# Retention layer: operands of the first two chunk steps made during the last block products, normalisation ahead of the state copy where heads change, and one residual load moved

## The chip, the cores and the metric

The program runs on one core of a Trainium2 chip. The metric is the device time of one execution in microseconds (us); lower is better. TensorE is written PE in the profile, its weight loads PEld, VectorE DVE, ScalarE ACT, GpSimd POOL; SyncE is SP, and it only issues transfers here. Each of these runs its own instructions in the order in which they stand in its queue, and an instruction that has to wait holds everything behind it on that engine. ACT issues a few transfers as well.

## The reference, cut to what matters

Two layers on a prompt of 1024 tokens and on 8 single decode tokens: a retention layer, then sliding-window attention. The change lies in the retention layer of the prompt, with 4 heads, keys of 256, values of 512 and chunks of 128 tokens (8 chunks a head):

```python
def step(S, inp):
    qc, kc, vc = inp
    inner = jnp.einsum('bthd,bshd->bhts', qc, kc) * dmask[None]
    o = jnp.einsum('bhts,bshe->bthe', inner, vc) \
        + jnp.einsum('bthd,bhde->bthe', qc, S) * cross_decay[None, :, :, None]
    S_new = S * chunk_decay[None, :, None, None] \
        + jnp.einsum('bshd,bshe->bhde', kc * k_decay[None, :, :, None], vc)
    return S_new, o
...
o = rmsnorm(o, g_out.reshape(RET_HEADS, RET_DV)).reshape(B, L, RET_V)
o = o * jax.nn.silu(gate)
return x + o @ w_out, S.astype(S0.dtype)
```

S starts at zero, so the first chunk of a head needs no product with the state.

## The kernel before, in words

All large products are in a split form: a float32 operand is a rounded part "h" and a remainder "l", and a product is three matmuls (h by h, h by l, l by h). Three stages follow one another.

**Block products (the input projection).** The projection to q, k, v and gate is made in a seven-product block scheme (`SEQ7`, L308). A list of slots gives PE's order: a slot is 12 matmuls of one block product (L330 to L332). `later(n, fn)` hangs work on slot n. The other engines evict each product (`evac`, L354 to L371), apply silu to the gate (L374), and SP spills q/k, v and gate to scratch in DRAM (`qks`, `vsc`, `gsc`; L387 is the spill of the gate). The last gate set passes through tiles named `raw`. Ten slots ahead of the end `b_first` (L750) issues the loads of q, v and gate of steps 0 and 1, of q of step 2, and of the masks.

**Chunk steps.** `steps` (L729) lists 32 steps: heads 0 and 1 in turn over their 8 chunks (steps 0 to 15), then heads 2 and 3. Steps 0, 1, 16 and 17 are first chunks (9 matmuls), the others have 15. The loop at L1052 writes, in round i: `b_qk(i+1)` (scores L859 and transposed keys L100 into a PSUM tile `tr`), `b_mm(i)` (state products L918 to L920 into `S`, output products L922 to L931 into `po`), the loads of q(i+3) and v(i+2), then `others(i)`, `b_tr(i-1)` (four transposes of the normalised output `on`, also into `tr`), and the load of gate(i+2). There are two `tr` tiles, used in turn.

`others(i)` (L1032) is the order of ACT, DVE and POOL: for step i-1 the state copies `b_Sh` (ACT, L938) and `b_Sl` (DVE, L950), then the norm `b_sq` (ACT, L957), `b_ts` (DVE, L961), `b_pw` (POOL, L115) and `b_on` (DVE, L969); for step i+1 the conversions `b_sT` (DVE), `b_vh` (ACT, L891), `b_kh` (ACT, L866), `b_kl` (DVE, L871), `b_sh` (ACT), `b_vl` (POOL, L896), `b_sl` (POOL); for step i-2 the gating `b_og` and the split `b_oh`/`b_ol`. After a head's last chunk `b_Sh` writes the final state to a tile `sf` (L942), which ACT sends to the output (L943).

Ahead of the loop SP issues `gbl(0)` and `gbl(1)`, the norm's gain rows of heads 0 and 1 (`gbh`, L996), and a mask `M23` (L1051). ACT issues `gbl(2)` and `gbl(3)` in rounds 16 and 17. The two `gbh` tiles and other tiles of this stage take memory in which the spilled `raw` tiles lay.

The last rounds also make the first output tile (128 features by 512 tokens) from its own weight rows (`b_w`, `b_wc`, `b_wmm`): 48 matmuls, L1024 to L1026, into a PSUM tile `S`.

**Output projection.** After `se.close()` (L1080) only PE's order is the written one; a scheduler places the instructions of SP, ACT, DVE and POOL. `wslot` (L1107) loads weights in pieces of 512 KB into two raw buffers `wr` (L1114), casts each on DVE to `wh` (L1121) and subtracts on POOL to `wl` (L1122). `ro_part` runs the matmuls L1179 to L1181 (12 for each piece in the first tiles). `ro_finish` (L1185) loads a tile of the residual x (`xr`, L1191), adds it to the product by transposing it into the same PSUM tile (L100), and writes x1 out. At the start stand `ro_ahead(2)` (the first four pieces) and `ro_finish(0, 0)`, which finishes the tile that the chunk stage made, and then the tile (1, 0).

Of the kernel before, what the change touches and what calls it, by code (L numbers as in the profile page):

```python
# [18 lines left out]
H = 4  # L19
# [51 lines left out]
def _trunk(ctx, tc, nc, a):  # L71
# [677 lines left out]

    def b_first():  # L750
# [98 lines left out]
    maskT = [M01[:, 0:128], M01[:, 128:256], M23[:, 0:128], M23[:, 128:256]]  # L849
    kdec = M01[:, 256:288].rearrange("p (h c) -> p h c", h=H)  # L850
    epsg = M01[:, 288:292]


    def b_qk(h, c):
        d = heads[h]
        qk = d["l", c][0]
        pt = d["pt", c] = trp.tile([128, 512], F32, name="tr")
        for f in range(2):
            mm(pt[:, :128], qk[:, 2 + f, :], qk[:, f, :], start=(f == 0), stop=(f == 1))  # L859
        for f in range(2):  # L860
            tr(pt[:, 128 + f * 128:256 + f * 128], qk[:, 2 + f, :], ident)

    def b_kh(h, c):
        d = heads[h]
        d["kh", c] = rp.tile([128, DK], F32R, name="kh", bufs=2)
        act(d["kh", c], d["pt", c][:, 128:384], AF.Copy, scale=kdec[:, h, c:c + 1])  # L866

    def b_kl(h, c):
        d = heads[h]
        d["kl", c] = rp.tile([128, DK], F32R, name="kl", bufs=2)  # L870
        dve.scalar_tensor_tensor(d["kl", c], d["pt", c][:, 128:384], kdec[:, h, c:c + 1], d["kh", c].bitcast(F32), MUL, SUB)  # L871

    def b_sT(h, c):
        d = heads[h]
        d["sT", c] = rp.tile([128, 128], F32, name="sT", bufs=2)
        dve.tensor_tensor(d["sT", c], d["pt", c][:, :128], maskT[h], MUL)

    def b_sh(h, c):
        d = heads[h]
        d["sh", c] = rp.tile([128, 128], F32R, name="sTh", bufs=2)  # L880
        act(d["sh", c], d["sT", c], AF.Copy)

    def b_sl(h, c):
        d = heads[h]
        d["sl", c] = rp.tile([128, 128], F32R, name="sTl", bufs=2)
        pool.tensor_tensor(d["sl", c], d["sT", c], d["sh", c].bitcast(F32), SUB)

    def b_vh(h, c):
        d = heads[h]
        d["vh", c] = rp.tile([128, DV], F32R, name="vh", bufs=2)  # L890
        act(d["vh", c], d["l", c][1], AF.Copy)  # L891

    def b_vl(h, c):
        d = heads[h]
        d["vl", c] = rp.tile([128, DV], F32R, name="vl", bufs=2)
        pool.tensor_tensor(d["vl", c], d["l", c][1], d["vh", c].bitcast(F32), SUB)  # L896

    def b_qh(h, c):
        d = heads[h]
        if c > 0:  # L900
            d["qh", c] = rp.tile([128, 2, 128], F32R, name="qh", bufs=2)
            dve.tensor_copy(d["qh", c], d["l", c][0][:, 0:2, :])

    def b_ql(h, c):
        d = heads[h]
        if c > 0:
            d["ql", c] = rp.tile([128, 2, 128], F32R, name="ql", bufs=2)
            pool.tensor_tensor(d["ql", c], d["l", c][0][:, 0:2, :], d["qh", c].bitcast(F32), SUB)
# [106 lines left out]

    def b_wmm(i):
# [11 lines left out]
    def at_step(fn, i):  # L1028
        if 0 <= i < len(steps):
            fn(*steps[i])  # L1030
# [21 lines left out]
    for i in range(-1, NS + 2):  # L1052
# [8 lines left out]
        if i in (NS - 2, NS - 1):  # L1061
            b_w(i - NS + 4)
# [872 lines left out]
```

## Time and profile before

| | |
|---|---|
| median of 3 runs | 1350.39 us (1350.27 to 1351.85) |
| the profiled execution | 1350.44 us, span 1348.6 us |
| mean granted TensorE clock | 0.995 |
| PE busy | 1308.8 us (97%) |
| PEld busy | 1222.4 us (91%) |
| POOL, DVE, ACT busy | 707.4, 701.1, 633.6 us |
| chunk stage and first output tile | from 542.8 to 703.6 us |

Positions are us from the start of the span. A timeline row gives start, duration, engine, line, operation, tile written and tiles read; a bracket at its end gives the engine's idle time ahead of it and what the profile takes for the releaser. A row with "SPq" or "ACTq" is the issue of a transfer, not the transfer. In a windows row each engine has its busy time and the number of its instructions; "PEclk" is the granted share of TensorE's clock, "DMA" the mean busy share of the 16 DMA engines.

### The profile page before, as it was taken

How to read it: one execution, taken by the hardware profiler on the slowest of the kernel's cores; microseconds unless marked ns; L12 is line 12 of the kernel's file. 1: busy time of each engine (PE TensorE's matmuls, PEld its weight loads, DVE VectorE, ACT ScalarE, POOL GpSimd, SP SyncE). 2: the span in 40 equal slices, each digit the busy share in tenths (PEclk: the TensorE clock that was granted, in tenths of full speed). 3: DMA queues.
4: the chain of work that ended last, by engine and by line, in shares of the span. 5: the costliest groups of instructions: out<-in, count | busy, mean ns of one | idle time of the engine just before them, and what ended most of it. 6: DMA issues, size and time to landing. Idle time of an engine off the chain costs nothing.

```text
span 1348.6 us, 25951 instructions
## 1 busy us (share of the span) xinstructions
PE 1308.8 (97%) x9661; PEld 1222.4 (91%) x9661; DVE 701.1 (52%) x1365; ACT 633.6 (47%) x1565; POOL 707.4 (52%) x825
## 2 busy tenths in 40 slices
PE   6999999999999999899999999998999999999998
PEld 6999999999999999787877899997889999998998
DVE  6943655656566553676752113335456555669321
ACT  5532444544455553677751112235465656656321
POOL 6653534435435543698977545454375666555000
PEclk9999999999999999999999999999999999999999
DMA  6314777587676753556556434442121111113532
GB/s 221 103 55 140 218 222 225 161 242 233 187 237 187 233 177 107 169 171 212 182 160 196 153 121 136 143 119 72 38 62 44 48 46 46 34 34 107 159 86 80
DMA packets 194771, 187.68 MB, mean 139 GB/s; under 512 B 12645, under 2 KB 174493, under 8 KB 194629
## 3 DMA queue, kind: packets, MB, share of 16 engines
q1 hardware_dynamic: 156576, 147.29, 35.9%
q10 hardware_dynamic: 38068, 38.73, 9.1%
q8 instruction: 76, 1.25, 0.4%
q14 instruction: 51, 0.41, 0.1%
HBM read 129.61 MB, written 57.41 MB: 139 GB/s over the span
## 4 chain that ended last, share of the span: by engine, by line
PE 85%; DVE 5%; POOL 4%; issue 3%; DMA 2%; ACT 1%; ACTq 0%; SPq 0%; POOLq 0%; DVEq 0%
PE b L330 7%; PE b L332 7%; PE b L331 7%; PE pj L1132 7%; PE pj L1134 6%; PE pj L1133 6%; PE b L323 4%; PE b L324 4%; PE b L325 4%; PE tr L100 4%; PE pj L1181 4%; PE pj L1179 4%; PE pj L1180 4%; PE o L1600 2%; POOL wl L1122 1%
## 5 line engine op out<-in xcount | busy, mean ns | idle before, releaser
L330 PE MATMUL b<-xh,woh 128*128 128x258 f32 x784 | 223.3, 285 | 0.0
L332 PE MATMUL b<-xh,wol 128*128 128x258 f32 x784 | 221.6, 283 | 0.0
L331 PE MATMUL b<-xl,woh 128*128 128x258 f32 x784 | 221.2, 282 | 0.0
L1132 PE MATMUL pj<-A_hi,wh 128*128 128x384 f32 (+1 forms) x512 | 178.7, 349 | 0.0
L1134 PE MATMUL pj<-A_hi,wl 128*128 128x384 f32 (+1 forms) x512 | 165.2, 323 | 0.0
L1133 PE MATMUL pj<-A_lo,wh 128*128 128x384 f32 (+1 forms) x512 | 165.1, 323 | 0.0
L330 PEld LDWEIGHTS b<-xh,woh 128*128 128x128 f32 x784 | 148.0, 189 | 4.1 <-issue 2.5
L331 PEld LDWEIGHTS b<-xl,woh 128*128 128x128 f32 x784 | 148.8, 190 | 0.0
L332 PEld LDWEIGHTS b<-xh,wol 128*128 128x128 f32 x784 | 148.1, 189 | 0.0
L221 POOL TENSOR_TENSOR wol<-raw,woh 128x512 fp32r<-128x512 f32 x52 | 68.5, 1325 | 139.7 <-ACT woh L216 139.0
L1122 POOL TENSOR_TENSOR wl<-wr,wh 128x1024 fp32r<-128x1024 f32 (+1 forms) x60 | 114.2, 1913 | 40.2 <-DVE wh L1121 19.5
L324 PE MATMUL b<-wol,xh 128*128 128x256 f32 x448 | 126.1, 281 | 0.3 <-DVE wol L221 0.3
L323 PE MATMUL b<-woh,xh 128*128 128x256 f32 x448 | 126.3, 282 | 0.0
L325 PE MATMUL b<-woh,xl 128*128 128x256 f32 x448 | 125.7, 281 | 0.0
L1132 PEld LDWEIGHTS pj<-A_hi,wh 128*128 128x128 f32 x512 | 97.3, 190 | 10.1 <-issue 9.4
L1133 PEld LDWEIGHTS pj<-A_lo,wh 128*128 128x128 f32 x512 | 97.6, 191 | 0.0
L1134 PEld LDWEIGHTS pj<-A_hi,wl 128*128 128x128 f32 x512 | 97.0, 190 | 0.0
L1577 POOL TENSOR_TENSOR s<-s,sm 128x512 f32<-128x512 f32 x64 | 68.9, 1077 | 49.7 <-DVE sm L1576 47.8
L323 PEld LDWEIGHTS b<-woh,xh 128*128 128x128 f32 x448 | 84.4, 188 | 2.5 <-issue 1.2
L324 PEld LDWEIGHTS b<-wol,xh 128*128 128x128 f32 x448 | 84.3, 188 | 0.8 <-DVE wol L221 0.8
L325 PEld LDWEIGHTS b<-woh,xl 128*128 128x128 f32 x448 | 84.3, 188 | 0.0
L1569 ACT ACTIVATE s<-s,mx 128x257 f32<-128x257 f32 x128 | 64.3, 505 | 30.2 <-DVE mx L1567 26.4
(379 smaller groups left out, 3564.7 us busy)
## 6 DMA issues: line engine op xcount, KB each, us to landing
raw<-in_w_in_ret_dram ACTq DMA_DIRECT2D x44, 512.0 KB
st<-in_state_ret_dram SPq DMA_DIRECT2D x64, 256.0 KB
out_dram<-st SPq DMA_DIRECT2D x64, 256.0 KB
wr<-in_w_out_ret_dram SPq DMA_DIRECT2D x32, 512.0 KB
wr<-in_w_in_swa_dram SPq DMA_DIRECT2D x18, 512.0 KB
vb<-vscr SPq DMA_DIRECT2D x64, 128.0 KB
evp<-qks SPq DMA_DIRECT2D x32, 256.0 KB
evx<-vsc SPq DMA_DIRECT2D x32, 256.0 KB
```

Of the source, the lines that this page charges most:

```text
L221: eng.tensor_tensor(lo, src_of(s, name, sub), hi.bitcast(F32), SUB)
L323: mm(dst, xh, wh, start=a and i == 0, stop=False, skip_group_check=True)
L324: mm(dst, xh, wl, start=False, stop=False, skip_group_check=True)
L325: mm(dst, xl, wh, start=False, stop=z, skip_group_check=True)
L330: mm(dst, wh, xh, start=a, stop=False, **sg)
L331: mm(dst, wh, xl, start=False, stop=False, **sg)
L332: mm(dst, wl, xh, start=False, stop=z, **sg)
L1122: lo_eng[0].tensor_tensor(lo[:, js, :], raw[:, i:i + step, :], hi.bitcast(F32)[:, js, :], ALU.subtract)
L1132: mm(ps, hi[:, k, fs], xh[:, k, t0:t1], start=first and k == ks[0], stop=False)
L1133: mm(ps, hi[:, k, fs], xl[:, k, t0:t1], start=False, stop=False)
L1134: mm(ps, lo[:, k, fs], xh[:, k, t0:t1], start=False, stop=last and k == ks[-1])
L1577: nc.gpsimd.tensor_tensor(st[:, :, 0:256], st[:, :, 0:256], sm.unsqueeze(2).broadcast_to([128, 2, 256]), ALU.mult)
```

## The change

Three edits, and helpers for the first.

1. `b_early(0)` and `b_early(1)` hang on the slots five and three ahead of the end of the block products. They issue the scores and transposes of steps 0 and 1 into PSUM banks of that stage, and all conversions of these steps into its SBUF buffers (tiles named `first`). The loop no longer makes them.
2. In `others`, the norm (`b_sq`, `b_ts`, `b_pw`) goes ahead of the state copies for the steps that are a head's last chunk, and for the first chunks of heads 2 and 3.
3. `b_x` loads the x tile of `ro_finish(0, 0)` in the last full round, into a buffer of ring "c"; its four transposes stand right behind the matmuls of the first output tile. `ro_finish(0, 0)` does neither any more.

```diff
+    def early(h, c):
+        return c == 0 and h < 2
+    def pt_tile(h, c):
+        if early(h, c):
+            return bank(0, h)
+        return rt[1].tile([128, 512], F32, name="tr")
+    def step_tile(h, c, n, dt_, name):
+        if not early(h, c):
+            return rt[0].tile([128, n], dt_, name=name, bufs=2)
+        if name == "sT":
+            return wq.tile([128, 512], F32, tag=("s1", "s2")[h], bufs=2, name="first")[:, 0:n]
+        key, a = dict(kh=("k", 0), kl=("k", 256), sTh=("s", 0), sTl=("s", 128)).get(name, (name, 0))
+        if (key, h) not in mk:
+            mk[key, h] = wq.tile([128, 512], F32R, tag="wop", bufs=12, name="first")
+        return mk[key, h][:, a:a + n]
...
+    CONV = (b_sT, b_qh, b_vh, b_kh, b_kl, b_sh, b_vl, b_sl, b_ql)
+    def b_early(i):
+        at_step(b_qk, i)
+        for fn in CONV:
+            at_step(fn, i)
...
     later(len(slots) - 10, b_first)
+    later(len(slots) - 5, b_early, 0)
+    later(len(slots) - 3, b_early, 1)
...
+    def b_x():
+        wo["x"] = ring("c")[:, 0:512].rearrange("p (c f) -> p c f", c=4)
+        nc.sync.dma_start(out=wo["x"], in_=x_prompt[0, 0:512, 0:128].rearrange("(c p) f -> p c f", p=128))
...
     def others(i):
-        for fn, n in ((b_og, i - 2), (b_Sh, i - 1), (b_Sl, i - 1), (b_sq, i - 1), (b_ts, i - 1), (b_pw, i - 1),
...
+        conv = [(fn, i + 1 if i + 1 > 1 else -1) for fn in CONV]
+        state = [(b_Sh, i - 1), (b_Sl, i - 1)]
+        norm = [(b_sq, i - 1), (b_ts, i - 1), (b_pw, i - 1)]
+        turn = 0 <= i - 1 < NS and (steps[i - 1][1] == NCH - 1 or (steps[i - 1][1] == 0 and i > 2))
+        for fn, n in ([(b_og, i - 2)] + (norm + state if turn else state + norm) + conv[0:3] +
+                      [(b_on, i - 1), (b_oh, i - 2)] + conv[3:7] + [(b_ol, i - 2)] + conv[7:]):
             at_step(fn, n)
...
     for i in range(-1, NS + 2):
-        at_step(b_qk, i + 1)
+        if i > 0:
+            at_step(b_qk, i + 1)
...
+        if i == NS - 1:
+            b_x()
...
+    for i in range(4):
+        tr(wo["ps"][:, i * 128:i * 128 + 128], wo["x"][:, i, :], ident, start=False, stop=(i == 3))
     sb.close()
     se.close()
...
-        xr = fp.tile([128, 4, 128], F32, name="xr", bufs=2)
...
+        if ft + gi:
+            xr = fp.tile([128, 4, 128], F32, name="xr", bufs=2)
...
```

The order on PE where the block products end and the chunk steps begin, before (`b` is a product's PSUM bank, `evp` holds q and k of a step):

```order
L332 MATMUL b_7286<-xh,wol 128x258
L859 MATMUL tr<-evp 128x128 x2
L100 MATMUL tr<-ident,evp 128x128 x2
L859 MATMUL tr<-evp 128x128 x2
L100 MATMUL tr<-ident,evp 128x128 x2
L918 MATMUL S<-vh,kh 128x512
```

The same place of the changed kernel, with the last matmul of the last block product first:

```order
L332 MATMUL b_7286<-xh,wol 128x258
L956 MATMUL S<-first 128x512
L957 MATMUL S<-first 128x512
L958 MATMUL S<-first 128x512
L956 MATMUL S<-first 128x512
L957 MATMUL S<-first 128x512
L958 MATMUL S<-first 128x512
L960 MATMUL po<-first 128x512
L961 MATMUL po<-first 128x512
L962 MATMUL po<-first 128x512
L777 MATMUL tr<-evp 128x128 x2
L100 MATMUL tr<-ident,evp 128x128 x2
```

The two pairs of scores and transposes have left this place; they stand among the products, the second pair with 24 product matmuls behind it.

The order on SP at the end of the chunk stage, before (L1004 loads the weights of the first output tile):

```order
L1004 DMA evx<-in_w_out_ret_dram 128x4x128 x2
L1114 DMA wr<-in_w_out_ret_dram 128x4x256 x2
L1191 DMA xr<-in_x_prompt_dram 128x4x128 x2
L1114 DMA wr<-in_w_out_ret_dram 128x4x256 x2
L1191 DMA xr<-in_x_prompt_dram 128x4x128
```

The same place after the change (L1056 is the load of `b_x`, L1238 the load in `ro_finish`, L1160 the load in `wslot`):

```order
L1042 DMA evx<-in_w_out_ret_dram 128x4x128 x2
L1056 DMA evc<-in_x_prompt_dram 128x4x128
L1238 DMA xr<-in_x_prompt_dram 128x4x128
L1160 DMA wr<-in_w_out_ret_dram 128x4x256 x2
L1238 DMA xr<-in_x_prompt_dram 128x4x128
L1160 DMA wr<-in_w_out_ret_dram 128x4x256 x6
```

The x load of tile (0, 0) is now L1056; the x load of tile (1, 0), which stood behind the first two weight pieces, stands ahead of them. It has the waits that the load of tile (0, 0) had before: for the last matmul of the first output tile and for the final states' transfers.

The order on ACT where heads 0 and 1 end (rounds 16 and 17), before:

```order
L996 DMA gbh<-in_ret_out_norm_dram 128x512
L942 ACTIVATE sf<-S 128x512 x2
L943 DMA out_dram<-sf 128x2x512
L957 ACTIVATE on,bss<-po 128x512
L891 ACTIVATE vh<-evx 128x512
L988 ACTIVATE B_hi<-og 128x4x128
L866 ACTIVATE kh<-tr,M_84 128x256
L881 ACTIVATE sTh<-sT 128x128
L996 DMA gbh<-in_ret_out_norm_dram 128x512
L938 ACTIVATE Sh<-S 128x512 x2
L957 ACTIVATE on,bss<-po 128x512
```

And after:

```order
L1034 DMA gbh<-in_ret_out_norm_dram 128x512
L995 ACTIVATE on,bss<-po 128x512
L980 ACTIVATE sf<-S 128x512 x2
L981 DMA out_dram<-sf 128x2x512
L809 ACTIVATE vh<-evx 128x512
L1026 ACTIVATE B_hi<-og 128x4x128
L784 ACTIVATE kh<-tr,M_84 128x256
L799 ACTIVATE sTh<-sT 128x128
L1034 DMA gbh<-in_ret_out_norm_dram 128x512
L995 ACTIVATE on,bss<-po 128x512
L976 ACTIVATE Sh<-S 128x512 x2
```

The square of the output has moved ahead of the two copies of the state, and ahead of the issue of the final state's transfer.

More of the change, by code (lines that the diff above doesn't have):

```diff
@@ new lines, in _trunk, with b_qk, b_kh @@
+    mk = {}
+    def b_qk(h, c):
+        d = heads[h]
+        qk = d["l", c][0]
+        pt = d["pt", c] = pt_tile(h, c)
+        for f in range(2):
+            mm(pt[:, :128], qk[:, 2 + f, :], qk[:, f, :], start=(f == 0), stop=(f == 1))
+        for f in range(2):
+            tr(pt[:, 128 + f * 128:256 + f * 128], qk[:, 2 + f, :], ident)
+    def b_kh(h, c):
+        d = heads[h]
+        d["kh", c] = step_tile(h, c, DK, F32R, "kh")
+        act(d["kh", c], d["pt", c][:, 128:384], AF.Copy, scale=mk["k"][:, h, c:c + 1])
@@ L848, in _trunk @@
     M23 = rp.tile([128, 256], F32, name="M23")
-    maskT = [M01[:, 0:128], M01[:, 128:256], M23[:, 0:128], M23[:, 128:256]]
-    kdec = M01[:, 256:288].rearrange("p (h c) -> p h c", h=H)
+    rt[:] = [rp, trp]
+    mk["m"] += [M23[:, 0:128], M23[:, 128:256]]
     epsg = M01[:, 288:292]
[L854 to L861, printed above, removed]
@@ L878, in b_sh @@
[L878 to L891, printed above, removed]
```

85 lines of the change are left out of this document (47 added, 38 removed).

## The prediction

> **What bounds the kernel now.** The page comes first: PE is busy for 97% of the span, so a stretch is worth only what PE stands still or runs slowly in it. The waits of PE from the end of the block products to the first output tiles come next.
>
> ```profile
> PE 1308.8 (97%) x9661; PEld 1222.4 (91%) x9661; DVE 701.1 (52%) x1365; ACT 633.6 (47%) x1565; POOL 707.4 (52%) x825
> ```
>
> ```profile
> PE S L100 <- DMA xr<-in_x_prompt_dram: 3.1, 1, 3.1
> PE tr L100 <- DVE on L969: 3.0, 3, 1.8
> PE S L918 <- ACT kh L866: 1.8, 1, 1.8
> PE tr L859 <- issue: 1.7, 2, 1.1
> PE S L919 <- POOL vl L896: 0.5, 1, 0.5
> ```
>
> In a row stand the instruction that waited, what released it, the total, the count and the longest. The three edits go for these rows: edit 1 for the last three (4.0 us), edit 2 for the second (3.0), edit 3 for the first (3.1). The rest of the working asks, place by place, what ends next. The sum is made against the profiled execution, 1350.44 us; the median of the three runs, 1350.39, is the same for this purpose, and so are the 1.8 us outside the span.
>
> **Edit 1: the start of the chunk steps.** These timeline rows carry the chain that ends in the scores of step 3.
>
> ```profile
> 543.26 0.42 ACT L374 ACTIVATE raw<-raw 128x258 f32<-128x258 f32 x1 [1.03 <-DVE raw L371]
> 545.65 0.29 DVE L876 TENSOR_TENSOR sT<-tr,M 128x128 f32<-128x128 f32 x1 [2.43 <-DMA gsc<-raw]
> 545.67 0.82 SPq L996 DMA_DIRECT2D gbh<-in_ret_out_norm_dram  x2
> 547.70 0.33 SPq L742 DMA_DIRECT2D evx<-vsc  x1
> 549.68 0.61 PE L859 MATMUL tr<-evp 128*128 128x128 f32 x4
> 550.27 0.48 PE L918 MATMUL S<-vh,kh 128*128 128x512 f32 x1
> 552.56 0.63 PE L100 MATMUL tr<-ident,on 128*128 128x128 f32 x4
> 552.71 0.63 ACT L891 ACTIVATE vh<-evx 128x512 fp32r<-128x512 f32 x1 [2.13 <-DMA evx<-vsc]
> 553.74 0.48 DVE L871 SCALAR_TENSOR_TENSOR kl<-tr,M,kh 128x256 fp32r<-128x256 f32 x1 [1.33 <-ACT kh L866]
> 554.32 0.68 PE L859 MATMUL tr<-evp 128*128 128x128 f32 x4 [1.14 <-issue]
> ```
>
> The last gate tile gets its silu at 543.26 and is spilled; the spill lands at 545.65. Only then may SP issue the gain rows into that memory (545.67), and behind them in SP's queue stand the second gain row, the mask, q of step 3 and v of step 2 (547.70). That v lands at 552.7, and vh, kh and kl of step 2 free the `tr` tile for the scores of step 3 at 554.32. None of this is an operand of steps 0 and 1. SP's order here is the same in the changed kernel, so the chain remains, and it hangs on the last product.
>
> That product now comes later: the two pairs of scores and transposes stand ahead of it on PE. A pair takes 550.27 - 549.68 = 0.59 us, and its scores 0.68 instead of 0.61 where PE starts on them out of a stand (554.32); I take 0.65 a pair, 1.3 for two. What they feed costs nothing on PE: ACT has three conversions of at most 0.63 us for a step, in slots in which it does 0.42 us and idles 1.03 (the row at 543.26). So last product, silu, spill, gain rows, v and the scores of step 3 all come 1.3 us later, at 555.6. Steps 0 and 1 themselves start early, at about 544.6, behind the last eviction (543.26 before), and with 552.56 - 550.27 = 2.3 us each and a pair between them end at about 549.8; PE then stands still, but for the transposes of step 0. The three waits of 4.0 us become one longer wait in front of step 3, and the 1.3 us moved forward is paid again at its end. **Term: +1.3** (1.0 to 1.4: v may be issued up to 0.26 us earlier, since 547.70 is also when POOL had done with its buffer, but the loads ahead of it already keep the DMA engines busy for 0.90 of 547 to 550, the last column but one).
>
> ```profile
> 547.00:550.00 3.00, 2.51 (x12) 1.93 (x12) 1.75 (x5) 2.39 (x6) 2.76 (x4) 1.00 0.90 215
> ```
>
> **The clock behind that wait.** The longer stand has a second price. Three windows of equal length, each with the one behind it, PE alone:
>
> ```profile
> 542.71:546.13 3.42, 1.62 (x13) 1.00 0.26 77
> 546.13:549.54 3.41, 2.32 (x9) 1.00 0.71 170
> 703.14:706.55 3.41, 0.44 (x2) 1.00 0.49 144
> 706.55:709.97 3.42, 3.27 (x10) 0.50 0.73 196
> 918.18:921.59 3.41, 1.59 (x11) 1.00 0.01 4
> 921.59:925.01 3.42, 3.21 (x13) 0.50 0.53 150
> ```
>
> With 0.44 us of work in 3.41 the clock was halved for the next window, with 1.59 once, with 1.62 not. In the changed kernel PE stands from about 549.8 to 555.6, but for 0.63 us of transposes when the gain row is there. Wherever the windows fall, one of them holds no more than about 1.2 us of work (0.63, and at worst 0.5 ahead of the stand), and the window behind it, at half clock, reaches over the restart by 0.8 us to its whole length, or a second one follows, and costs half of that. **Term: +1.4** (0.4 to 2.4). The Trainium skill, "TensorE: Matmul & The Clock Gate", Part 1, has the gate fall to half after at least one idle window of about 3.4 us, free-running. By an idle window taken strictly, with the transposes in the middle of the stand hardly any phase has a window without work, and this term would be near zero; the row 703.14 to 706.55, not wholly idle, speaks for the wider reading.
>
> **Edit 2: where heads 0 and 1 end.**
>
> ```profile
> 618.04 0.60 PE L100 MATMUL tr<-ident,on 128*128 128x128 f32 x4
> 619.82 0.60 ACT L957 ACTIVATE on<-po 128x512 f32<-128x512 f32 x1 [0.55 <-POOL sTl L886]
> 622.38 0.63 PE L100 MATMUL tr<-ident,on 128*128 128x128 f32 x4 [1.02 <-DVE on L969]
> 623.33 0.35 ACTq L996 DMA_DIRECT2D gbh<-in_ret_out_norm_dram  x1
> 627.50 0.63 PE L100 MATMUL tr<-ident,on 128*128 128x128 f32 x4 [1.76 <-DVE on L969]
> ```
>
> The square of step 15 sits behind the state copy and the issue of its transfer in ACT's queue, though its product ends when PE starts the transposes at 618.04. Moved ahead, it starts 1.6 us sooner, which is more than the 1.02 us that PE waits: that wait goes. At step 16 the square comes ahead of the state copies, but DVE's `on` still stands behind DVE's own two state copies, which wait for ACT's; so the 1.76 us stays, relative to PE. **Term: -1.0** (-1.4 to +0.3: the upper end if a load for steps 17 and 18 comes no sooner than before).
>
> **Edit 3: the first output tile.**
>
> ```profile
> 691.03 1.41 SPq L1114 DMA_DIRECT2D wr<-in_w_out_ret_dram  x2
> 703.19 0.40 PE L1026 MATMUL S<-A_hi,wol 128*128 128x512 f32 x1
> 703.49 4.64 POOL L1122 TENSOR_TENSOR wl<-wr,wh 128x1024 fp32r<-128x1024 f32 x2 [2.27 <-PE S L1025]
> 703.66 0.92 SPq L1191 DMA_DIRECT2D xr<-in_x_prompt_dram  x2
> 705.85 2.67 SPq L1114 DMA_DIRECT2D wr<-in_w_out_ret_dram  x2
> 706.70 1.09 PE L100 MATMUL S<-ident,xr 128*128 128x128 f32 x4 [3.12 <-DMA xr<-in_x_prompt_dram]
> 708.43 0.63 PE L1181 MATMUL pj<-A_hi,wl 128*128 128x512 f32 x1
> 709.48 0.69 DVE L1121 CAST wh<-wr 128x1024 fp32r<-128x1024 f32 x1 [9.41 <-DMA wr<-in_w_out_ret_dram]
> 710.25 2.40 POOL L1122 TENSOR_TENSOR wl<-wr,wh 128x1024 fp32r<-128x1024 f32 x1 [2.13 <-DVE wh L1121]
> 727.25 2.38 POOL L1122 TENSOR_TENSOR wl<-wr,wh 128x1024 fp32r<-128x1024 f32 x1 [0.63 <-DVE wh L1121]
> 729.69 0.50 PE L1181 MATMUL pj<-A_hi,wl 128*128 128x512 f32 x1 [0.46 <-POOL wl L1122]
> ```
>
> PE's 3.12 us for x and the half clock behind it (half of the 3.27 us of work at 0.50, 1.6 us) look like the gain. But a second chain runs from 703.5 to 729.7: POOL's `wl` frees a raw buffer, the next piece is loaded (705.85 to 709.48), cast (0.7), subtracted (2.4). Its first two pieces are done at about 705.8 and 708.1 (two in 4.64 us), its third at 712.65, its eighth at 729.63, and there PE waits again, 0.46 us. PE has caught up with this chain by then, for all its 4.7 us. So removing the x wait alone gains 0.46 us at most.
>
> The chain itself now starts later. Before, its first two pieces were issued at 691.03, and POOL could start on them as soon as L1025 was done. In the changed SP queue they stand behind the x load of the next tile, which waits for the last matmul L1026 (703.6). So x goes at 703.66, the pieces at about 704.1 and 704.6; with 3.6 us for the first (705.85 to 709.48) and a little for the x ahead of it, it lands at about 708, and 0.7 + 2.4 us later, at 711.2, the first `wl` is done, where it was at 705.8. From the first to the eighth is 23.85 us (705.8 to 729.63) in the trace. Carried over whole, the eighth ends at 735.0, +5.4; with three round trips like the first (first to third piece, 6.85 us) and one more subtraction of 2.4, at 734.1, +4.5; if PE alone set the pace, from the first L1181 at 711.2 instead of 708.43, +2.8. I take the second, since the same two buffers go round. **Term: +4.5** (2.8 to 5.4). From 730 on PE has no wait in which to win this back: the next tiles reuse these weights.
>
> **Sum:** 1350.44 + 1.3 + 1.4 - 1.0 + 4.5 = **1356.6 us**.
>
> **The rivals.** *The start comes out clean* (not slower). If v of step 2 came as early as before or sooner, because the gain rows do not hold it, the 4.0 us of waits would shrink to the 0.6 of the last eviction (the lesser of the two in the row of 1.7), and the clock would stay. Terms: -3.4 + 0 - 1.0 + 4.5, 1350.5 us, no change. For it: steps 0 and 1 no longer need anything that is late. Against it: 2.13 us of ACT's wait before 552.71 is for that v, and nothing ahead of it on SP has moved. It decides if v lands before about 550. *The weight chain is not late* (faster). If the first pieces were on the chip when the first tile ends, the x wait and its half clock would be saved as far as the eighth piece lets them; with a chain that keeps pace this is up to 3.1 + 1.6 us. With the start as forecast: 1350.44 + 1.3 + 1.4 - 1.0 - 4.7 = 1347.4. Against it: SP's order. *The clock stays full* behind the wait at step 3, because a halving needs a window with no work at all: 1356.6 - 1.4 = 1355.2. For it: the window at 542.71 with 1.62 us of work did not halve. Against it: the one at 703.14 with 0.44 us did. *The change does not take the work off the place*: PE's order shows that it does.
>
> **How the numbers follow.** The forecast with its terms has 0.60, and the same with the clock at full 0.15; a clean start 0.10; a chain that is not late 0.08; the rest, 0.07, is a mishap among these that costs more, such as products waiting for the early conversions. A measurement tells about 0.2%, 2.7 us, from no change. The clean start lies within it, and so does a forecast whose terms all come out low (1350.44 + 1.0 + 0.4 - 1.4 + 2.8 = 1353.2): same 0.14. Faster 0.09, slower 0.77. The upper ends give 1350.44 + 1.4 + 2.4 + 0.3 + 5.4 = 1359.9. The range is 1351.5 to 1360.0: below lie the chain that is not late and most of the clean start, and the mishaps reach a little above.
>
> **What would show it.** The scores of step 3 start some 11 us behind the last silu (554.32 - 543.26 before), with one wait of more than 3 us ahead of them, for kl of step 2 or the v behind it; a half-clock window follows. The wait at tr of step 15 is gone, that of step 16 is there. The first weight pieces are issued only after the last L1026, DVE's first cast falls after 707, and PE waits for `wh` where it waited for x, and again for `wl` before the end of the eighth piece. It is wrong if the pieces are issued near 692, if v of step 2 lands within 8 us of that silu, or if PE's total idle time between 543 and 735 falls below the 10.1 us that the five rows of waits add up to.

## The result and the profile after

The changed kernel is slower: 1364.09 us median of 4 runs (1361.72 to 1366.32), against 1350.33 of 4 runs before (1348.51 to 1351.85). The ratio is 1.0099 with a 95% interval of 1.0087 to 1.0112. The profiled execution took 1361.72 us with a span of 1359.7, so the two profiled executions lie 11.3 us apart, 11.1 of it in the span; the other 2.5 us of the medians' 13.8 lie between runs. The page's first block and PE's waits, from 535 to 740 us:

```profile
PE 1314.1 (97%) x9661; PEld 1224.8 (90%) x9661; DVE 700.2 (51%) x1365; ACT 631.0 (46%) x1565; POOL 707.2 (52%) x825
```

```profile
PE pj L1225 <- DVE wh L1167: 5.4, 1, 5.4
PE tr L777 <- DVE kl L789: 3.9, 1, 3.9
PE pj L1227 <- POOL wl L1168: 2.9, 3, 1.2
PE tr L100 <- DVE on L1007: 1.9, 3, 1.5
PE tr L777 <- PE tr L100: 1.7, 2, 0.9
PE S L956 <- DVE raw L371: 0.6, 1, 0.6
```

The same number of matmuls takes 5.3 us longer. An estimate from the windows at half clock gives 3.4 of it: 10.0 us of work ran at half clock between 535 and 740 us, and 3.3 before. The listed waits are 16.4 us; before they were 10.6, the five rows of the prediction and 0.5 for POOL's remainder of the eighth weight piece. The three rows that the edits went for are gone or smaller, and each has a successor: `kl` of step 2 stands where the start waited, `wh` where x was waited for, and `wl` behind it. Where the time came in is read from the same four instructions in both kernels.

| position in the span | before | after | moved so far |
|---|---|---|---|
| last silu of the block products (L374) | 543.26 | 544.95 | +1.7 |
| scores of step 3 | 554.32 | 556.11 | +1.8 |
| last matmul of the first output tile starts | 703.19 | 706.91 | +3.7 |
| first matmul of the eighth weight piece's remainder | 729.69 | 740.60 | +10.9 |
| end of span | 1348.6 | 1359.7 | +11.1 |

**The start.** Timeline rows of the changed kernel, the chain that ends in the scores of step 3:

```profile
544.95 0.42 ACT L374 ACTIVATE raw<-raw 128x258 f32<-128x258 f32 x1 [0.92 <-DVE raw L371]
547.35 0.82 SPq L1034 DMA_DIRECT2D gbh<-in_ret_out_norm_dram  x2
549.17 0.43 SPq L742 DMA_DIRECT2D evx<-vsc  x1
551.59 0.66 PE L100 MATMUL tr<-ident,on 128*128 128x128 f32 x4 [1.49 <-DVE on L1007]
554.50 0.63 ACT L809 ACTIVATE vh<-evx 128x512 fp32r<-128x512 f32 x1 [5.39 <-DMA evx<-vsc]
555.52 0.48 DVE L789 SCALAR_TENSOR_TENSOR kl<-tr,M,kh 128x256 fp32r<-128x256 f32 x1 [4.00 <-ACT kh L784]
556.11 1.19 PE L777 MATMUL tr<-evp 128*128 128x128 f32 x4 [3.87 <-DVE kl L789]
```

It is the chain of before, link by link: silu, spill, gain rows, v, vh, kl, scores, 11.16 us from the first to the last row (11.06 before). PE does steps 0 and 1 early and then stands. Behind it the clock, in windows of PE alone:

```profile
551.47:554.88 3.41, 0.66 (x4) 1.00 0.96 331
554.88:558.29 3.41, 2.18 (x8) 0.50 0.34 132
558.29:561.71 3.42, 3.42 (x9) 0.50 0.68 229
561.71:565.12 3.41, 3.41 (x21) 1.00 0.49 155
```

0.66 us of work, the transposes of step 0, stands in the first window, and two windows at half clock follow, not one. In the first of these PE still stands until 556.11, so that it works for 2.18 us of it.

**The turn of the heads.** PE's three waits there, timeline rows:

```profile
626.93 0.68 PE L777 MATMUL tr<-evp 128*128 128x128 f32 x4 [0.83 <-PE tr L100]
630.10 0.63 PE L100 MATMUL tr<-ident,on 128*128 128x128 f32 x4 [0.21 <-DVE on L1007]
631.60 0.68 PE L777 MATMUL tr<-evp 128*128 128x128 f32 x4 [0.87 <-PE tr L100]
```

They sum to 1.91 us where 1.02 + 1.76 = 2.78 stood. The waits for `on` are nearly gone; scores that wait for a free `tr` tile took part of their place.

**The first output tiles.** Timeline rows of the end of the chunk stage and the weight chain:

```profile
706.91 0.40 PE L1068 MATMUL S<-A_hi,wol 128*128 128x512 f32 x1
707.39 0.37 SPq L1238 DMA_DIRECT2D xr<-in_x_prompt_dram  x1
707.81 1.05 SPq L1160 DMA_DIRECT2D wr<-in_w_out_ret_dram  x2
712.39 0.69 DVE L1167 CAST wh<-wr 128x1024 fp32r<-128x1024 f32 x1 [9.98 <-DMA wr<-in_w_out_ret_dram]
713.14 0.79 PE L1225 MATMUL pj<-A_hi,wh 128*128 128x512 f32 x1 [5.39 <-DVE wh L1167]
713.16 2.35 POOL L1168 TENSOR_TENSOR wl<-wr,wh 128x1024 fp32r<-128x1024 f32 x1 [8.72 <-DVE wh L1167]
715.54 3.36 SPq L1160 DMA_DIRECT2D wr<-in_w_out_ret_dram  x2
720.06 0.69 DVE L1167 CAST wh<-wr 128x1024 fp32r<-128x1024 f32 x1 [4.00 <-DMA wr<-in_w_out_ret_dram]
740.60 0.50 PE L1227 MATMUL pj<-A_hi,wl 128*128 128x512 f32 x1 [0.41 <-POOL wl L1168]
```

The first two pieces, issued at 691.03 before, are issued at 707.81, behind the next x load (707.39), which waits for the last matmul. The first piece lands 4.6 us later (712.39 - 707.81), PE waits 5.39 us for its cast, and at the eighth piece it still waits for POOL.

### The profile page after: what moved, and what is told of

Its sections match the earlier page's. It is cut to its first block, busy times and chain, and to the rows that moved or that the text cites. A ratio compares the mean times of both kernels' runs of the same rounds, so it can differ in the third digit from the quotient of the medians.

```text
span 1359.7 us, 25941 instructions
## 1 busy us (share of the span) xinstructions
PE 1314.1 (97%) x9661; PEld 1224.8 (90%) x9661; DVE 700.2 (51%) x1365; ACT 631.0 (46%) x1565; POOL 707.2 (52%) x825
## 4 chain that ended last, share of the span: by engine, by line
PE 85%; DVE 5%; POOL 4%; DMA 3%; issue 2%; ACT 2%; SPq 0%; ACTq 0%; DVEq 0%; POOLq 0%
PE b L330 7%; PE b L332 7%; PE b L331 7%; PE pj L1178 6%; PE pj L1179 6%; PE pj L1180 6%; PE b L323 4%; PE b L324 4%; PE b L325 4%; PE tr L100 4%; PE pj L1227 4%; PE pj L1225 4%; PE pj L1226 4%; PE o L1647 2%; DMA wr<-in_w_out_ret_dram 1%
```

## The experiments

The theory at the start was that of the forecast: the x load ahead of the weight pieces on SP holds them back. The first four runs take the change apart; what they showed led to the others. One measure goes through all of them: the distance from the end of the last matmul of the first output tile to the first matmul on the eighth piece's remainder. It is 703.59 to 729.69 = 26.1 us before and 707.31 to 740.60 = 33.3 after. No experiment but those with fill matmuls does other arithmetic than the changed kernel, and what the fills write is overwritten by the next use of the tile.

### Edit 1 alone

```diff
-        turn = 0 <= i - 1 < NS and (...)
+        turn = False
...
-        if i == NS - 1:
-            b_x()
...
-        if ft + gi:
+        if True:
```

> Edit 1 alone (operands of steps 0 and 1 under the last block products), without the moved norm and without the moved x load. SP's queue at the end of the chunk stage has the order of before: two weight pieces, then x. Theory: taking these steps' tiles out of the chunk stage's pool also shifts which memory the later tiles get, so that the first weight piece now lies over the remainder weights of the first output tile and has to wait for their last matmul; then the loss at the first output tiles is there without edit 3: start +1.7, half clock +2.8, weights about +7, together about 1362 us, with the first wr issued behind the last matmul of the first output tile. Rival: the weights are held by the place of the x load in SP's queue alone; then only the start and the clock are lost, about 1355 us, with the first wr issued some 12 us ahead of that matmul.

Measured: 1362.59 us, ratio 1.0074 (1.0061 to 1.0087). SP's first issue of weight pieces and PE's wait for x, timeline rows:

```profile
706.31 0.92 SPq L1152 DMA_DIRECT2D wr<-in_w_out_ret_dram  x2
712.44 1.09 PE L100 MATMUL S<-ident,xr 128*128 128x128 f32 x4 [5.92 <-DMA xr<-in_x_prompt_dram]
```

What SP waited for ahead of a weight piece at this place, before the change and with edit 1 alone:

```profile
SPq L1114 <- PE po L931: 3.6, 1, 3.6
```

```profile
SPq L1152 <- PE S L1064: 7.0, 1, 7.0
```

The pieces stand ahead of every x load on SP here, as they did before, and are issued at 706.31 all the same, right at the end of the first tile's last matmul (706.12 + 0.40); before they were issued 12.6 us ahead of that point. So SP's order is not the only thing that holds them. Edit 1 takes steps 0 and 1's tiles out of the chunk stage's pool, and every tile that the pool hands out later lies elsewhere. The releaser of the issue is now L1064, the product of the first output tile that reads the remainder of that tile's own weights; before, it was an output product of the last chunk step (PE po L931, last started at 690.84). The distance is 32.6 us, and the time is the one expected.

### Edit 2 alone

```diff
+        state = [(b_Sh, i - 1), (b_Sl, i - 1)]
+        norm = [(b_sq, i - 1), (b_ts, i - 1), (b_pw, i - 1)]
+        turn = 0 <= i - 1 < NS and (...)
+        for fn, n in ([(b_og, i - 2)] + (norm + state if turn else state + norm) + ...
```

> Edit 2 alone (norm ahead of the state copies where heads begin and end). Theory: the wait of 1.0 us at the transposes of step 15 goes and nothing takes its place, about 1349.4 us. Rival: the waits only move to other steps, 1350.3 us.

Measured: 1351.66 us, ratio 1.0005 (0.9990 to 1.0019). PE's waits at the turn are 1.14 + 0.18 us where they were 1.02 + 1.76, and from the scores of step 3 to the last matmul of the first output tile it takes 147.60 us where it took 148.87: 1.3 us less, near the forecast's term. The medians don't show it, so they decide neither for the theory nor for its rival; with an interval of 3.9 us they could not tell 1 us from nothing.

### Edit 3 alone

Kernel before with `b_x`, its four transposes and the condition in `ro_finish`:

```diff
+        if i == NS - 1:
+            b_x()
...
+    for i in range(4):
+        tr(wo["ps"][:, i * 128:i * 128 + 128], wo["x"][:, i, :], ident, start=False, stop=(i == 3))
...
+        if ft + gi:
```

> Edit 3 alone (x of the first output tile loaded early). The pool's tiles lie as before, but the x load of the next tile stands ahead of the first two weight pieces in SP's queue and waits for the last matmul of the first output tile. Theory: the queue alone holds the weights as well, so the x wait is replaced by a wait for wh and the eighth piece ends some 7 us later: about 1357 us. Rival: the loss at this place in the changed kernel came from the memory layout alone; then the x wait and its half clock are saved as far as the eighth piece allows, about 1350 us or a little less.

Measured: 1361.19 us, ratio 1.0058 (1.0044 to 1.0073). SP's issues:

```profile
706.14 0.37 SPq L1200 DMA_DIRECT2D xr<-in_x_prompt_dram  x1
706.57 1.05 SPq L1122 DMA_DIRECT2D wr<-in_w_out_ret_dram  x2
```

The chunk stage's pool is that of before here, so SP's order by itself holds the pieces until x has gone, and PE waits 6.1 us for `wh`. The distance is 34.8 us, and the time 4 us above the one expected. This profile also shows that an unchanged stretch does not always run alike: up to the first output tile the two kernels are the same, and yet there are two half windows here that the profile before does not have. One lies at the start of the chunk steps (547.45 to 550.86), where the profile of edit 2 alone has one too (548.52 to 551.94), and one follows the turn of the heads. Windows of PE, edit 3 alone:

```profile
625.00:630.00 5.00, 2.69 (x16) 0.94 0.67 252
630.00:635.00 5.00, 5.00 (x19) 0.72 0.52 159
```

The first tile's last matmul so ends 2.5 us later than before (706.07); the distance, which begins there, does not count that. Edits 1 and 3 each delay the same load, which fits that 0.74% and 0.58% together make only 0.99%.

### The weights ahead of x

The changed kernel, with the x loads of tiles (1, 0) and (2, 0) on ACT's queue, so that nothing stands ahead of the pieces on SP:

```diff
-            nc.sync.dma_start(out=xr[:, 0:nfull, :], ...
+            (nc.scalar if gi == 0 and ft in (1, 2) else nc.sync).dma_start(out=xr[:, 0:nfull, :], ...
```

> The changed kernel with the x loads of tiles (1, 0) and (2, 0) issued by ACT, so that nothing that waits stands ahead of the weight pieces in SP's queue. Theory (memory layout holds them too): the first piece still waits for nearly the last matmul of the first output tile, 0.4 us earlier than in the changed kernel at most: about 1363 us. Rival (queue order alone): the pieces are issued some 12 us before that matmul and the loss of 7 us is gone, about 1357 us.

Measured: 1359.67 us, ratio 1.0053 (1.0039 to 1.0067), distance 31.7. The issue on SP:

```profile
707.04 0.92 SPq L1160 DMA_DIRECT2D wr<-in_w_out_ret_dram  x2
```

The time lies between the two that were expected; the profiled execution, 1362.76 us, is the slowest of the six. The place in memory holds the issue, as with edit 1 alone. What is gained is the landing: the cast starts at 710.53, 3.5 us behind the issue, instead of 4.6. This goes with the order of issue and not with the queue, since with edit 1 alone, where both x loads follow the pieces on SP, it is 3.6 (706.31 to 709.87), and with edit 3 alone, where an x load goes ahead of them, 5.3 (706.57 to 711.84). In the changed kernel the DMA share (last column but one) shows the engines full while x and the pieces are in flight:

```profile
711.00:712.00 1.00, 0.00 (x0) 0.96 0.99 335
712.00:713.00 1.00, 0.00 (x0) 0.50 0.99 341
```

### Edit 1 alone, with the places of before

Edit 1 alone, and two unused tiles each of the names that steps 0 and 1 took from the pool before, taken once and never written, so that all later tiles lie where they lay before. No engine's instructions change.

```diff
+    for _ in range(2):
+        rp.tile([128, DV], F32, name="gbh", bufs=2)
+    for _ in range(2):
+        for n_, w_, t_ in (("sT", 128, F32), ("vh", DV, F32R), ("kh", DK, F32R), ("kl", DK, F32R),
+                           ("sTh", 128, F32R), ("vl", DV, F32R), ("sTl", 128, F32R)):
+            rp.tile([128, w_], t_, name=n_, bufs=2)
```

> Edit 1 alone, with the unused tiles that restore the memory places, and nothing else. The instructions and their order are those of the run with edit 1 alone; only addresses differ. Theory: the first weight pieces are issued ahead of the end of the first output tile again, the x wait is 3 us as before, and 7 us of the loss of that run (1362.6) go: 1355 us. Rival: addresses do not matter, and the loss comes from weights that PE and POOL reach late for another reason: 1362 us.

Measured: 1356.75 us, ratio 1.0033 (1.0020 to 1.0046), 5.8 us under edit 1 alone. Issue of the pieces and PE's wait for x:

```profile
694.66 1.41 SPq L1158 DMA_DIRECT2D wr<-in_w_out_ret_dram  x2
710.30 0.63 PE L100 MATMUL S<-ident,xr 128*128 128x128 f32 x4 [3.08 <-DMA xr<-in_x_prompt_dram]
```

The pieces go 12.6 us ahead of the tile's end again, the wait for x is 3.08 as before (3.12), and the distance is 26.0, that of before. With the same instructions in the same order, only the places differ: this shows that the places held the weights. What is left, 0.33%, is edit 1's start at these places; the same kernel, run once more below, has 0.17%.

### Both holds taken away

The weights-ahead kernel with the same unused tiles.

> The changed kernel with both causes of the late weights taken away: tiles that nobody uses are allocated in the chunk stage's pool in the place of those of steps 0 and 1, so that all later tiles get the memory they had before, and the x loads of tiles (1, 0) and (2, 0) are issued by ACT. Theory: the first weight pieces are issued some 12 us ahead of the end of the first output tile, PE's wait for wh and the x wait are both gone, and what remains is the start (+1.7), its half clock (+2 to +4) and the moved norm (-1): 1353 to 1355 us. Rival: the weights are late for a third reason; then about 1360 us as in the run with only the x loads moved.

Measured: 1358.24 us, ratio 1.0049 (1.0037 to 1.0061), distance 29.5. SP's issue and DVE's first cast:

```profile
694.82 16.93 SPq L1166 DMA_DIRECT2D wr<-in_w_out_ret_dram  x3
```

```profile
707.86 1.29 DVE L1173 CAST wh<-wr 128x1024 fp32r<-128x1024 f32 x2 [5.31 <-PE S L100]
```

The pieces are on the chip early, and yet the distance is 3.4 us longer than before. The cast now waits for the transposes of x (5.31 us, released by PE L100): edit 3's x tile, in ring "c", is what they read, so it lies under the first `wh`. POOL's first remainder so starts behind x's transposes, where before it started while PE was still waiting for x; it is done 4.0 us behind the tile's end, before 2.2. That is 1.8 of the 3.4 us. Another 1.3 is the landing of the third piece, 4.9 us behind its issue (711.38 to 716.26) where it was 3.6. The start moved too: the transposes of step 0 wait 3.16 us, because the unused tiles put `Sl`, DVE's remainder copy of the state, over operands of the early steps (its releaser is the last product of step 1, PE po L968). The expected time was missed on both counts, and the rival, a third reason, came nearer.

### v of step 2 and q of step 3 early

The last kernel, with these two loads issued ahead of the gain rows.

```diff
+    later(len(slots) - 1, b_v, 2)
+    later(len(slots) - 1, b_q, 3)
...
+            if i > 0:
-            b_q(i + 3)
-            b_v(i + 2)
+                b_q(i + 3)
+                b_v(i + 2)
```

> The run before, and v of step 2 and q of step 3 are loaded in the last slot of the block products, ahead of the last spills and so ahead of the gain rows. Theory: the wait of 3.9 us ahead of the scores of step 3 was that load, standing behind the gain rows that wait for the last spill; it shrinks to under 1 us, no half-clock window follows, and the time is 6 to 7 us under the run before, about 1348 us, under the kernel before. Rival: the gain row of head 0, which the norm of step 0 needs, holds PE at the transposes of step 0 and the next scores nearly as long; then the gain is 2 us or less.

Measured: 1354.30 us, ratio 1.0027 (1.0017 to 1.0037), 3.9 us under the one it was made from, where 6 to 7 were expected. The profiled execution, 1357.76 us, is the slowest of its twelve. The scores of step 3 no longer wait: they stand at 554.12, straight behind the transposes of step 0 (553.27), where the changed kernel has 556.11. So the v behind the gain rows is what the scores of step 3 waited for, as the forecast said. The wait of 3.16 us at the transposes remains, for the reason given above, and one half window follows it (553.38 to 556.79), which the forecast had ruled out.

### Filling the wait at step 3

Edit 1 alone with the places of before, with seven matmuls into a spare `po` tile ahead of the scores of step 3.

```diff
+    def b_fill():
+        po = fillpo["po"] = spp.tile([128, DV], F32, name="po", bufs=2)
+        for _ in range(7):
+            mm(po[:, 0:288], ident, M01[:, 0:288], start=True, stop=True)
```

> The run before with seven matmuls of 0.48 us that feed nothing put into PE's wait ahead of the scores of step 3. They end before the scores are released, so the wait itself keeps its length. Theory: the clock halves behind the wait because PE does nothing in it; with the filling it stays at full for the next windows, and the time falls by 2 to 3.4 us, to about 1352.5 us. Rival: at half clock the chunk steps were held by the other engines anyway, and the time stays at that of the run before.

Measured: 1356.87 us, ratio 1.0044 (1.0027 to 1.0060). Timeline:

```profile
553.94 5.01 PE L959 MATMUL po<-M,ident 128*128 128x288 f32 x14
```

The fill itself ran largely at half clock (0.50 from 553.45 to 556.86), behind the wait of 3.16 us that was left open, and reached past the release (scores at 558.78 instead of 556.06). It says nothing on the price of the clock.

### Filling both waits, beside the same kernel without

Six such matmuls ahead of the transposes of step 0 and four ahead of the scores of step 3.

```diff
+        if (h, c) == (0, 0):
+            for _ in range(6):
+                mm(pt[:, 0:288], ident, M01[:, 0:288], start=True, stop=True)
...
+        if i == 2:
+            b_fill(4)
```

> Edit 1 alone at the old memory places again, with idle PE time filled in both waits of the start: six matmuls of 0.48 us into the wait ahead of the transposes of step 0 and four into the one ahead of the scores of step 3. In the earlier run with filling only the second wait was filled; the clock was already halved there by the first, and the filling itself ran at half speed and past the release. Theory: with both filled the clock stays at full through 565 us, the scores of step 3 start at 556 as without filling, and PE reaches the end of the first output tile 2 to 3 us earlier than without it (707.2 in the profile). Rival: no half window goes, or PE is held by the other engines there; then PE reaches it at the same time.

> Edit 1 alone at the old memory places, without filling, once more, on the same chip as the run before and as its counterpart. Theory: 2 to 3 us over the run with both waits filled, near 1356 us. Rival: the same time as that run.

Measured: with fill 1354.88 us, ratio 1.0017 (1.0001 to 1.0033), without 1354.94, ratio 1.0017 (1.0005 to 1.0029). Windows of PE with the fill:

```profile
551.00:554.00 3.00, 2.75 (x14) 1.00 0.91 301
554.00:557.00 3.00, 2.70 (x15) 1.00 0.62 238
```

And without:

```profile
554.00:557.00 3.00, 0.92 (x4) 0.69 0.66 253
557.00:560.00 3.00, 3.00 (x10) 0.50 0.36 128
```

With nearly the same scores of step 3 (555.84 and 556.08), the last matmul of the first tile starts at 704.30 with the fill and at 707.91 without: 148.46 us against 151.83. Less the waits at the turn (2.52 and 3.20), the clock's share is 2.7 us in these profiles, and against the earlier profile of the kernel without fill (150.76, waits 2.76) 2.1. The medians are equal, where 2 to 3 us were expected between them, and the two kernels' runs spread over 10.2 and 6.5 us. So the price is read from one trace of each kernel, and the medians do not show it.

### All of it at once, with two layouts

The weights-ahead kernel with the early v and q, and unused tiles in two orders, the second chosen so that nothing of steps 0 and 1 and nothing of the first output tile's weights lies under what comes next.

```diff
+    for _ in range(2):
+        rp.tile([128, DV], F32, name="og", bufs=2)
...
+    for _ in range(2):
+        rp.tile([128, DV], F32, name="on", bufs=2)
```

> The changed kernel with all the losses taken away that the runs have shown: v of step 2 and q of step 3 loaded ahead of the last spills, unused tiles that put the gain rows and the state copies over memory that is free early and keep the first weight piece off the last products' operands, and the x loads of tiles (1, 0) and (2, 0) on ACT. Theory: the gain rows are issued right behind the last spill instead of behind its landing, PE's waits at the start shrink to about 1.5 us in all, no half-clock window follows, and the time is 3 to 5 us under the run with only v moved (1354.3): about 1350 us, level with the kernel before or a little under it. Rival: the gain row lands no sooner because the DMA engines are busy with the spills; then 1353 us.

> As the run with all losses taken away, but with another set of unused tiles. In that run PE still waited 3.2 us at the transposes of step 0: DVE's first remainder copy of the state lay over the operands of step 1 and waited for their last matmul, and everything behind it on DVE with it. Here neither the gain rows nor the state copies nor what DVE does for step 0 lies over anything that is read late, and the first weight piece lies over a tile that is free some 10 us ahead of the end of the first output tile. Theory: memory places were what was left: PE waits under 2 us in all at the start, the scores of step 3 start at 552 or sooner (554.3 in the kernel before), no half-clock window follows, and the time is 1346 to 1350 us, under the kernel before. Rival: the gain row lands no earlier than 551 since the DMA engines are taken by the spills and the loads, or the clock halves all the same; then 1352 us or more.

Measured: the first layout 1356.23 us, ratio 1.0028 (1.0015 to 1.0041), the second 1351.75, ratio 0.9997 (0.9985 to 1.0009). In the first, DVE's state copy lies over operands of step 1 and holds what stands behind it:

```profile
550.04 1.29 DVE L1012 SCALAR_TENSOR_TENSOR Sl<-S,Sh 128x512 fp32r<-128x512 f32 x2 [5.29 <-PE po L986]
553.10 1.11 PE L100 MATMUL tr<-ident,on 128*128 128x128 f32 x4 [3.16 <-DVE on L1031]
```

In the second it does not, and the start is what the change could have given:

```profile
551.73 0.66 PE L100 MATMUL tr<-ident,on 128*128 128x128 f32 x4 [1.78 <-DVE on L1041]
552.22 0.61 PE L777 MATMUL tr<-evp 128*128 128x128 f32 x4
704.36 0.80 PE L1262 MATMUL pj<-A_hi,wl 128*128 128x512 f32 x1 [2.08 <-POOL wl L1203]
```

```profile
700.81 1.30 DVE L1202 CAST wh<-wr 128x1024 fp32r<-128x1024 f32 x2 [5.31 <-PE S L100]
```

The scores of step 3 stand at 552.22 (554.32 before), no half window follows, and the first tile's last matmul, just ahead of x's transposes, ends 3.3 us earlier than before (700.34 against 703.59). But the first cast still waits for x's transposes (700.81), the distance is 29.3 where it was 26.1, and the eighth piece's matmul stands at 729.63, before at 729.69. The gain of the start is given back at the weight chain to the last tenth. This kernel is level with the one before (the changed one has a ratio of 1.0099), but not under it, as was expected of it; the first layout missed its expected time too. Nothing tried here beats the kernel before, and no run moved the x tile away from under the first `wh`.

## Why the prediction was right or wrong

The direction and the places were right: each of the four terms came in where the text put it and with its sign. The sum was too small, 6.2 us against 11.3 in the profiled executions, and the time lay above the range. Two steps failed: the clock term paid for half of one window where two followed, and the weights term took the chain behind the late pieces to be shorter than it was.

- **Start, forecast +1.3, measured +1.4.** The chain was the one named, and moved as a whole; the run with the early v took away its last link. The last silu came 1.69 us later, but only 1.33 of it is the edit's. Counted back from the last product matmul of the block stage, the fiftieth, ahead of both early pairs, already starts 0.35 us later (536.93 against 536.58), and a hundred us earlier it is the same 0.35 (444.02 against 443.67); edits 2 and 3 alone, which leave this stage as it was, stand there 0.17 and 0.29 behind. From there on each pair adds 0.58 us and the products next to them the rest. So the sum of 1.3 for two pairs was right, and 0.35 of the table's +1.8 is a difference between two executions.
- **Clock, forecast +1.4, measured about +2.8.** From the scores of step 3 to the first tile's last matmul the changed kernel lost 1.93 us while the turn gained 0.87, so 2.8 are left. The step that failed is that half of one window is paid: two windows of 3.41 us followed one another. "Or a second one follows" stood beside it as a choice, not as an addition, and the upper end was 2.4. The traces of this case show when a second one came. In all of them together, between 535 and 760 us, a half window with 1.22 to 2.49 us of work was followed by another (12 cases), and one with 2.92 us or more was not (25 cases); later in the span the two are not so cleanly apart. PE stood still for the first 1.2 us of the first half window and worked for 2.2, which goes with a second one by these counts. The pair of kernels with and without fill gives 2.1 to 2.7. The kernel before was also lucky here: its own start had 1.62 us of work in a window and kept the clock, and the same start lost a half window in the profiles of edits 2 and 3 alone, with 1.13 and 1.58. The rival of a clock that stays full is out: 0.66 us of work in the window 551.47 to 554.88 did not keep it. The Trainium skill, "TensorE: Matmul & The Clock Gate", Part 1, asks for an idle window; taken strictly, as a window without any work, the trace disagrees, and a window with 0.66 us counted as idle.
- **Turn, forecast -1.0, measured -0.9** (-1.3 in edit 2 alone). The mechanism held at step 15. At step 16 the wait did not stay 1.76 as written: it fell to 0.21, and waits for the `tr` tile of 0.83 and 0.87 came in. Each ends 0.1 us behind the `kl` that reads this tile (ends at 626.83 and 631.49); for the second, `vh` of step 18 had waited 1.40 us for its load (629.47), which is the condition that the text gave for its upper end.
- **Weights, forecast +4.5 (2.8 to 5.4), measured +7.2** (33.3 - 26.1). This term was mis-sized, above its own upper bound. The first remainder was done 8.2 us behind the tile's end (713.16 + 2.35 - 707.31), where the working gives 7.6 (711.2 - 703.6): behind an x load the first piece landed in 4.6 us, and the working allows 3.9 (704.1 to 708). From there to the eighth remainder the text took 22.9 us, and it took 25.0 (to 740.55, the end of POOL's row ahead of 740.60). The first round trip took 7.9 instead of 6.85 because the third piece landed in 4.5 us (715.54 to 720.06) instead of 3.6, and the last step, taken for one subtraction of 2.4, took 3.5; it took 3.7 before as well, so the working could have read it. 0.6 + 2.1 make the 2.7 missing.
- **Why the third piece landed late** was not asked in any run, but the traces hold a candidate. Behind the other engines' end one of the sixteen DMA engines still moves the piece (a share of 0.06 from 718.50 to 719.50). A transfer of 16 KB on the queue that the profile names "instruction" starts 1.0 us behind the issue of that piece. In all eight profiles with a late third piece (4.5 to 5.6 us) it starts 1.0 to 1.8 us behind that issue, in the six others (3.4 to 3.8 us) 2.8 to 3.2 us. That it is the cause is not shown, since no run moved it.
- **The cause of the weights term was half of it.** The working had SP's order as the only hold. Edit 3 alone shows that this is enough; edit 1 alone, that edit 1 holds the same load through the places of its tiles, which no step of the prediction looked at; and the kernel with both holds gone, a third, x's tile under `wh`. That kernel's distance is 3.4 us longer than before (29.5 against 26.1), of which 1.8 is the later first remainder. This third hold is read from its releaser; no run took it away. The working's remark that removing the x wait gains 0.46 us at most pointed the right way: removing it cost.
- **The rivals.** The clean start did not happen in the changed kernel. With v issued ahead of the gain rows, the condition the text gave, it came only in the second layout (waits of 0.61 and 1.78 us, no half window); in the kernel with v alone moved, a wait of 3.16 us and a half window stayed. A weight chain that is not late was reached in no kernel that has edit 3; edit 1 with the places of before has it, and the wait for x with it.

Open: the medians lie 2.5 us further apart than the profiles. The mean granted clock was 0.995 in the profile of before and 0.991 after, and the profiles of edits 2 and 3 alone show that a half window can come in one execution behind waits that brought none in another. More of them in the timed runs of the changed kernel would fit, but no trace of those runs shows them.

## What to carry to other kernels

When tiles move from one pool to another, ask for each later tile what lies under it now: a load far behind the edit can come to wait for a reader that it had nothing to do with, and neither the order of instructions nor the diff shows it. Of every load that is moved or dropped, look at what comes to stand behind the remaining ones on that queue; here one waiting load moved two weight pieces from 12.6 us ahead of the tile's end to 0.5 us behind it (edit 3 alone). Before taking away a wait, see whether a second chain ends just behind it, because then the gain is only the difference between the two.

## What the runs showed of the hardware

- Two half-clock windows in a row, 6.8 us, followed waits of 1.49 and 3.87 us with 0.66 us of work between them. The same came behind the 5.39 us wait at the weights, with 1.22 us of work in the first of the two; before, a wait of 3.12 brought one, with 3.27 us of work in it:

```profile
708.40:711.81 3.41, 0.00 (x0) 1.00 0.92 277
711.81:715.22 3.41, 1.22 (x2) 0.52 0.79 261
715.22:718.63 3.41, 3.06 (x7) 0.50 0.48 153
```

- The work in a window does not say sharply whether the clock halves behind it. A window with 1.58 us (544.03 to 547.45, edit 3 alone) was followed by a half window, and one with 1.42 us (630.23 to 633.64, the kernel without fill) was not.
- The first weight piece lands 3.5 or 3.6 us behind its issue with the x loads issued behind it, on the other queue or on the same one, and 4.6 or 5.3 us with an x load just ahead of the two pieces and one just behind them, the DMA engines at a share of about 1.0 meanwhile.
- Fill matmuls kept the clock where they covered both waits of the stretch, and not where one was left open: seven behind an open wait of 3.16 us took 5.01 us at mostly half clock, and ten over both waits (3.07 + 2.11 us) kept it at full. One profile shows each.
